# An encoder's SwiGLU by seven products (Strassen): another order of the products, each partial sum copied out

## The chip, the cores and the metric

The kernel runs on one core of a Trainium2 chip. The metric is the device time of one execution in microseconds (us), the median of several runs. TensorE (PE) does matmuls, VectorE (DVE) and ScalarE (ACT) work element by element, GpSimd (POOL) fills buffers, SyncE (SP) issues nearly all loads. Each engine works through its own list of instructions in order and waits for the others by semaphores.

## The reference

Two layers on x of 512 positions by 1024, in float32. Each layer has a mixer (eight retention heads and four differential-attention heads) and a SwiGLU; the change is in the latter.

```python
for l in range(DEPTH):                      # DEPTH = 2
    h = rms_norm(x, attn_norm_g[l])
    proj = h @ w_in[l]                      # 1024 -> 3584
    ...                                     # retention heads, attention heads
    x = x + jnp.concatenate([ret, da], axis=-1) @ w_out[l]

    h = rms_norm(x, ffn_norm_g[l])
    x = x + (jax.nn.silu(h @ w_gate[l]) * (h @ w_up[l])) @ w_down[l]   # 1024 -> 2816 -> 1024
return x
```

## The kernel before, in words

**Two parts for each number.** Matmuls run on float32 rounded to `F32R`. To keep the precision, each operand is split into `hi` (a cast on ACT) and `lo` (the rest, a subtraction on DVE), and a product takes three matmuls: hi by hi, hi by lo, lo by hi. `mm3` (lines 197 to 200) does so for 512 columns. Weights are loaded by SP into one of three `raw` buffers, then split into one of three pairs of buffers with the tags `hi` and `lo` (`NHL = 3`, `parts`, line 171).

**The SwiGLU.** Positions lie along the columns (two halves, H1 and H2, of C = 256 columns each), features along the 128 partitions. The 2816 inner features are 22 units of 128. Groups of units are listed in `FFN` (line 34): after the gate and up products of a group, its part of w_down is applied in a *sweep* over the eight output tiles (`for m in range(KT)`, line 785), and each is added to x (`residual`, line 626). The activations of a group's units are kept till its sweep is done, as pairs in buffers of the tags `h`, `mix` or `rn`.

**Plain units** (the group (0, 4)): `gate_up` computes gate and up with `mm3`. After each, `combine(i)` computes for two of the eight contraction tiles the sums and differences that the seven products need of the normed x, and splits them: b11, b21, b22, t1 to t4. They stay in buffers of `mix`, `qk`, `w` and `dv` to the layer's end.

**Seven-product units** (all others): `seven` treats gate and up of a unit as a 2 by 2 block matrix (gate and up; first and second half of the 1024 contraction rows), times a 2 by 2 block matrix (halves of the contraction; halves of the columns). Seven block products instead of eight are done. The weights come as two loads, `a` (g1 and u2) and `b` (g2 and u1). DVE makes four differences from them: s3 and s1 (in one buffer, s31), s2 and s4 (s24). All are split: s31, then `a`, then g2, then s24. A product is twelve matmuls of 256 columns (`product`, line 736): four contraction tiles by three. The sums run up in three banks of PSUM: `pa` takes g1, s2, s3 and u2 on top of each other, `pb` takes g2, `pc` takes s1 and then s4. What `pa` holds in between is needed too, so ACT and DVE read it (lines 747 to 755) before the next product goes on top. `seven` is a generator; the loop at line 778 interleaves one unit's steps with the next one's by its `yield`s.

**What sets the order.** The kernel is built with `schedule_with_timeline_sim=True`: a planner puts each engine's instructions into an order before the run, by the order of the program, by its own idea of when inputs are ready, and by which buffers are free; it hands the buffers of a tag out. So the order on PE is near to the one written, but products are interleaved. On the chip the order is fixed.

Of the kernel before, what the change touches and what calls it, by code (L numbers as in the profile page):

```python
# [30 lines left out]
FIRST = [("dk", 0), ("dq", 0), ("dk", 1), ("dq", 1)]  # L31
SINGLE = [(n, m) for n in ("dk", "dq") for m in (2, 3)] + [(n, m) for n in ("rk", "rq", "rg") for m in range(4)]

FFN = [(0, 4), (4, 9), (9, 14), (14, 18), (18, FT)]
PLAIN = FFN[0][1]

PAIRS = [0, 0, 1, 0, 1, 2, 0, 1, 2, 3, 1, 2, 3, 2, 3, 3]
# [9 lines left out]
PRM_N = 88  # L47

CST_DIST, CST_DPOS, CST_DNEG, CST_QPOS = 0, 896, 1280, 1664
CST_ID, CST_ONES, CST_BONES, CST_KPOS = 2176, 2304, 2432, 2560  # L50
CST_N = 2564


@with_exitstack
def encoder_kernel(ctx: ExitStack, tc: tile.TileContext, xT, wfirst, wsingle, wvv, wout, wgu, wdn, prm, lam, cst, outT):
# [11 lines left out]
    def nm(s):  # L67
        uid[0] += 1
        return f"{s}{uid[0]}"
# [76 lines left out]
        return sq  # L146

    def round_ones():
        for n, o in (("ones_r", CST_ONES), ("bones_r", CST_BONES)):
            consts[n] = cpool.tile([P, P], F32R, name=n)  # L150
            nc.vector.tensor_copy(consts[n], cst_sb[:, o : o + P])

    eps_sb = cpool.tile([P, 1], F32, name="eps_sb")
    nc.vector.memset(eps_sb, EPS)
# [39 lines left out]
    def chunk(*a, **kw):  # L194
        return split_chunk(*load_chunk(*a, **kw))
# [69 lines left out]
    def prepare_small():  # L265
        lg = cpool.tile([P, 48], F32, name="lg")
        func(lg, prm_sb[:, PRM_DEC : PRM_DEC + 48], AF.Exp)
        nc.vector.tensor_scalar(lg, lg, -1.0, None, op0=ALU.mult)
        lam_sb = big("lam")
        nc.sync.dma_start(lam_sb, lam)  # L270
        lamn = cpool.tile([P, DEPTH], F32, name="lamn")
        for l in range(DEPTH):
            dots = small("dots", 2)
            for i in range(2):
                o = l * 4 * HD + 2 * i * HD
                prod = spool.tile([P, HD], F32, tag="prod", name=nm("prod"), bufs=2)
                nc.vector.tensor_tensor_reduce(prod, lam_sb[:, o : o + HD], lam_sb[:, o + HD : o + 2 * HD], 1.0, 0.0, ALU.mult, ALU.add, dots[:, i : i + 1])
            ex = small("lamex", 2)
            func(ex, dots, AF.Exp)

            nc.vector.tensor_scalar(lamn[:, l : l + 1], ex[:, 1:2], ex[:, 0:1], -LAM_INIT[l], op0=ALU.subtract, op1=ALU.add)
        gq = cpool.tile([P, DEPTH, DH], F32, name="gq")
        gd = cpool.tile([P, DEPTH], F32, name="gd")
        for l in range(DEPTH):
            for h in range(DH):
                nc.vector.tensor_scalar(gq[:, l, h : h + 1], prm_sb[:, PRM_QG + l : PRM_QG + l + 1], -0.5 * HD ** -0.5 / SLOPES[h], None, op0=ALU.mult)
            nc.vector.tensor_scalar(gd[:, l : l + 1], prm_sb[:, PRM_DG + l : PRM_DG + l + 1], 1.0 - LAM_INIT[l], None, op0=ALU.mult)
        wk = cpool.tile([P, DEPTH, 4, RH], F32, name="wk")
# [12 lines left out]

    def layer(l, n1, h, x_src, first_raw):
# [410 lines left out]
        def split_in(raw, hi, lo, n=1024):  # L713
            nc.scalar.copy(hi, raw[:, :n])  # L714
            nc.vector.tensor_tensor(lo, raw[:, :n], f32(hi), op=ALU.subtract)  # L715
            return [(hi[:, i * T : (i + 1) * T], lo[:, i * T : (i + 1) * T]) for i in range(n // T)]
# [4 lines left out]
        def seven(ff, act, tag, bufs):  # L721
            a, b = load_chunk(wgu[l, ff, 0])[0], load_chunk(wgu[l, ff, 1])[0]
            s31, s24 = (tpool.tile([P, 1024], F32, tag="ah", name=nm("s"), bufs=NAH) for _ in range(2))
            u1 = b[:, T:]
            nc.vector.tensor_tensor(s31[:, :T], u1, a[:, :T], op=ALU.subtract)
            nc.vector.tensor_tensor(s31[:, T:], u1, a[:, T:], op=ALU.subtract)  # L726
            nc.vector.tensor_tensor(s24[:, :T], a[:, :T], s31[:, T:], op=ALU.subtract)
            nc.vector.tensor_tensor(s24[:, T:], b[:, :T], s24[:, :T], op=ALU.subtract)
            s3, s1 = split_in(s31, *parts())
            g1, u2 = split_in(a, *parts())  # L730
            (g2,) = split_in(b, big("g2h", F32R), big("g2l", F32R), T)
            s2, s4 = split_in(s24, wide(), wide())

            pa, pb, pc = (bank() for bank in (acc_bank, sc_bank, out_bank))

            def product(ps, w, r, start):
                for k in range(4):
                    L, R = cut(w, slice(None), slice(k * P, (k + 1) * P)), comb[k][r]
                    for i, (x1, x2) in enumerate(((0, 0), (0, 1), (1, 0))):
                        nc.tensor.matmul(ps[:, :C], L[x1], R[x2], start=start and k + i == 0, stop=k == 3 and i == 2, skip_group_check=True)  # L740

            g, u, v = big("g"), big("u"), big("v")
            product(pc, s1, "t1", True)
            yield
            product(pa, g1, "b11", True)
            product(pb, g2, "b21", True)
            nc.scalar.copy(v[:, H1], pb[:, :C])
            nc.vector.tensor_tensor(g[:, H1], pa[:, :C], v[:, H1], op=ALU.add)  # L748
            yield
            product(pa, s2, "t2", False)  # L750
            nc.scalar.copy(v[:, H2], pa[:, :C])  # L751
            yield
            product(pa, s3, "t3", False)
            nc.scalar.copy(u[:, H1], pa[:, :C])
            nc.vector.tensor_tensor(u[:, H2], pc[:, :C], u[:, H1], op=ALU.add)
            yield
            product(pa, u2, "t4", False)
            product(pc, s4, "b22", False)
            nc.vector.tensor_tensor(g[:, H2], pc[:, :C], v[:, H2], op=ALU.add)  # L759
            func(g, g, AF.Silu)  # L760
            nc.vector.tensor_tensor(u[:, H1], pa[:, :C], g[:, H1], op=ALU.mult)  # L761
            nc.vector.tensor_tensor(u[:, H2], u[:, H2], g[:, H2], op=ALU.mult)
            act.append(split(u, tag, bufs))

        for a0, a1 in FFN:
            act, last = [], a1 == FT
            if a1 <= PLAIN:
                for ff in range(a0, a1):
                    act.append(gate_up(ff, *(("mix", NMIX) if ff < 2 else ("rn", 4))))
                    combine(ff)  # L770
            else:
                units = []
                for ff in range(a0, a1):
                    tag = ("h", 8) if not last else ("mix", NMIX) if ff < a0 + 2 else ("rn", 4)
                    units.append(seven(ff, act, *tag))
                next(units[0])
                next(units[0])
                for i, unit in enumerate(units):
                    then = units[i + 1] if i + 1 < len(units) else iter([0, 0])
                    next(unit)  # L780
                    next(then)
                    next(unit)
                    next(then)
                    next(unit, None)
            for m in range(KT):
                w = chunk(wdn[l, m][:, a0 * P : a1 * P], (a1 - a0) * P)
                if last and l + 1 == DEPTH and m == KT - 1:

                    for t, queue in ((H1, nc.sync), (H2, nc.scalar)):
# [9 lines left out]
                if last and l + 1 < DEPTH:  # L799
                    residual(m, x[m], ps, n3, h3, PRM_AG + 8 * (l + 1))  # L800
                    nc.sync.dma_start(xscr[m], x[m])
                else:
                    residual(m, x[m], ps, None, None, None)
                    if last:
                        nc.sync.dma_start(outT[m], x[m])
        return n3, h3
# [15 lines left out]
def _constants():  # L822
    import numpy as np

    p = np.arange(P, dtype=np.float32)[:, None]
    ndist = -np.abs(p + 384 - np.arange(896, dtype=np.float32)[None])
    d = np.arange(384, dtype=np.float32)[None] - P - p
    j = np.arange(C, dtype=np.float32)
    qpos = np.tile(np.concatenate([C - j, j + 1])[None], (P, 1))
    blk = (np.arange(P) // HD)[:, None] == (np.arange(P) // HD)[None]  # L830
    kpos = np.concatenate([C - 1 - p, C - 1 - P - p, p, P + p], 1)
    return np.concatenate(
        [ndist, np.maximum(d, 0), np.maximum(-d, 0), qpos, np.eye(P), np.ones((P, P)), blk, kpos], 1
    ).astype(np.float32)


# [74 lines left out]
```

## Time and profile before

| | |
|---|---|
| median of 3 runs | 1313.53 us (1311.27 to 1313.73) |
| the profiled execution: its time, its span | 1314.86 us, 1313.1 us |
| PE, DVE, ACT, POOL busy, share of the span | 96%, 74%, 52%, 1% |
| granted TensorE clock, mean | 0.996 |
| DMA moved, mean rate | 120.30 MB, 92 GB/s |
| layer 0: plain units and start of their sweep | 294.5 to 347.3 us |
| layer 0: groups of seven-product units with their sweeps | 347.3 to 637.7 us |
| layer 1: the same two | 944.0 to 998.2 us, 998.2 to 1290.6 us |

A row of the timeline reads: start, duration, engine, line of the kernel, operation, what is written <- what is read, shapes, count, and in brackets how long the engine had been idle before and who ended it. The records of matmuls overlap: one starts while the one before is drained, so the distance between two starts says what a matmul costs. A row of the waits view reads: who waited, for whom, total us, times, longest. In windows: busy us of each engine, its instructions, granted clock, share of DMA, GB/s.

### The profile page before, as it was taken

To read this page: it belongs to the slowest core of one execution; us is meant where nothing else is said; L and a number is where in the kernel's file an instruction comes from. 1 tells how busy PE (TensorE), PEld (TensorE's weight loads), DVE (VectorE), ACT (ScalarE), POOL (GpSimd) and SP (SyncE) were. 2 spreads that over 40 slices of the span, in tenths; PEclk is the share of its full clock that TensorE was granted. 3 is DMA by queue.
4 is the path that set the end of the run, shared out by engine and by line. 5 is a ranking of instruction groups with operands and counts; after the bars stand their busy time and mean duration, and the time that the engine had idled before them with its cause. 6 is when DMAs were issued, how large, how long until landed. Compare 5 with 4: busy or idle time off the path is not lost.

```text
span 1313.1 us, 19158 instructions
## 1 busy us (share of the span) xinstructions
PE 1263.8 (96%) x7516; PEld 1100.5 (84%) x7516; DVE 972.4 (74%) x1634; ACT 683.4 (52%) x1138; POOL 17.3 (1%) x38
## 2 busy tenths in 40 slices
PE   9999999999899999998999999999999999999998
PEld 8888998778797888988888888977878889888787
DVE  6899769779874766767659988686897757566664
ACT  6878656455343443434548875654653434334342
POOL 1000000000000000000000000000000000000000
PEclk9999999999999999999999999999999999999999
DMA  7212224122323324232443122230314233232323
GB/s 269 86 49 81 65 67 126 49 68 74 116 85 92 97 73 121 73 105 80 144 130 92 37 85 76 88 106 32 105 40 133 79 95 113 61 116 66 113 74 103
DMA packets 41562, 120.30 MB, mean 92 GB/s; under 512 B 4736, under 2 KB 4992, under 8 KB 41344
## 3 DMA queue, kind: packets, MB, share of 16 engines
q1 hardware_dynamic: 41040, 118.64, 29.1%
q8 instruction: 59, 0.97, 0.3%
q10 hardware_dynamic: 432, 0.44, 0.1%
q14 instruction: 31, 0.25, 0.1%
HBM read 114.87 MB, written 4.19 MB: 91 GB/s over the span
## 4 chain that ended last, share of the span: by engine, by line
PE 38%; DVE 6%; DMA 3%; ACT 2%; issue 2%; DVEq 0%; ACTq 0%; SPq 0%
PE acc L740 6%; PE acc L198 5%; PE acc L199 5%; PE acc L200 5%; DMA raw<-in_wgu 3%; PE o L740 3%; PE o L198 2%; PE o L199 2%; PE o L200 2%; PE sc L198 2%; PE sc L199 1%; PE sc L200 1%; PE sc L392 1%; PE sc L740 1%; DVE lo L715 1%
## 5 line engine op out<-in xcount | busy, mean ns | idle before, releaser
L187 ACT CAST hi<-raw 128x1024 fp32r<-128x1024 f32 (+2 forms) x171 | 143.4, 850 | 185.0 <-PE acc L199 53.4
L191 DVE TENSOR_TENSOR lo<-raw,hi 128x1024 fp32r<-128x1024 f32 (+2 forms) x172 | 166.2, 972 | 69.9 <-ACT hi L187 69.2
L198 PE MATMUL acc<-h,hi 128*128 128x512 f32 x411 | 161.8, 395 | 0.7 <-DVE u L761 0.4
L199 PE MATMUL acc<-h,hi 128*128 128x512 f32 x411 | 161.0, 392 | 0.0
L200 PE MATMUL acc<-h,lo 128*128 128x512 f32 x411 | 160.7, 392 | 0.0
L198 PEld LDWEIGHTS acc<-h,hi 128*128 128x128 f32 x411 | 77.1, 188 | 19.8 <-ACT hi L187 2.4
L200 PEld LDWEIGHTS acc<-h,lo 128*128 128x128 f32 x411 | 77.2, 188 | 16.0
L199 PEld LDWEIGHTS acc<-h,hi 128*128 128x128 f32 x411 | 77.2, 188 | 15.5 <-DVE h L216 0.4
L740 PE MATMUL acc<-hi,hi 128*128 128x256 f32 x288 | 83.3, 289 | 2.1 <-ACT v L751 2.0
L740 PE MATMUL acc<-lo,hi 128*128 128x256 f32 x288 | 81.3, 282 | 0.0
L740 PE MATMUL acc<-hi,lo 128*128 128x256 f32 x288 | 81.2, 282 | 0.0
L106 ACT ACTIVATE g<-g 128x512 f32<-128x512 f32 x44 | 27.8, 632 | 83.6 <-DVE g L759 81.8
L740 PE MATMUL acc<-hi,s 128*128 128x256 f32 x288 | 61.2, 295 | 7.4 <-DVE g L748 7.4
L714 ACT CAST hi<-s 128x1024 fp32r<-128x1024 f32 x36 | 37.8, 1051 | 55.3 <-DVE s L726 34.2
L715 DVE TENSOR_TENSOR lo<-raw,hi 128x1024 fp32r<-128x1024 f32 x36 | 43.9, 1220 | 27.8 <-ACT hi L714 27.8
L714 ACT CAST hi<-raw 128x1024 fp32r<-128x1024 f32 x36 | 37.7, 1048 | 51.5 <-issue 29.5
L740 PE MATMUL acc<-bh,hi 128*128 128x256 f32 x144 | 43.6, 303 | 17.0 <-ACT hi L714 17.0
L740 PEld LDWEIGHTS acc<-hi,hi 128*128 128x128 f32 x288 | 54.6, 190 | 5.1 <-ACT v L751 4.6
L198 PE MATMUL sc<-h,hi 128*128 128x512 f32 x147 | 57.7, 396 | 0.6 <-ACT h L215 0.6
L740 PE MATMUL o<-b,s 128*128 128x256 f32 x432 | 57.6, 283 | 0.0
L199 PE MATMUL sc<-h,hi 128*128 128x512 f32 x147 | 57.4, 391 | 0.0
L200 PE MATMUL sc<-h,lo 128*128 128x512 f32 x147 | 57.1, 390 | 0.0
(234 smaller groups left out, 3694.2 us busy)
## 6 DMA issues: line engine op xcount, KB each, us to landing
raw<-in_wgu SPq DMA_DIRECT2D x88, 512.0 KB, 3.6
raw<-in_wsingle SPq DMA_DIRECT2D x32, 512.0 KB, 3.6
raw<-in_wdn SPq DMA_DIRECT2D x48, 256.0 KB, 2.7
raw<-in_wdn SPq DMA_DIRECT2D x32, 320.0 KB, 2.9
raw<-in_wvv SPq DMA_DIRECT2D x16, 512.0 KB, 3.7
raw<-in_wout SPq DMA_DIRECT2D x16, 512.0 KB, 3.6
x<-in_xT SPq DMA_DIRECT2D x15, 256.0 KB, 4.3
raw<-in_wfirst SPq DMA_DIRECT2D x8, 256.0 KB, 5.1
```

The source lines that it names most:

```text
L106: i = nc.scalar.activation(out, src, f, **kw).ins
L187: c = nc.scalar.copy(hi[:, s], raw[:, s])
L191: nc.vector.tensor_tensor(lo[:, s], raw[:, s], f32(hi[:, s]), op=ALU.subtract)
L198: nc.tensor.matmul(out, L[0], R[0], start=start, stop=False)
L199: nc.tensor.matmul(out, L[0], R[1], start=False, stop=False)
L200: nc.tensor.matmul(out, L[1], R[0], start=False, stop=stop)
L392: nc.tensor.matmul(ps, q[m][:, t], k[m][part], start=part == 0, stop=part == 1)
L714: nc.scalar.copy(hi, raw[:, :n])
L715: nc.vector.tensor_tensor(lo, raw[:, :n], f32(hi), op=ALU.subtract)
L740: nc.tensor.matmul(ps[:, :C], L[x1], R[x2], start=start and k + i == 0, stop=k == 3 and i == 2, skip_group_check=True)
```

## The change

- The groups are (0, 4), (4, 12), (12, 18), (18, 22) instead of (0, 4), (4, 9), (9, 14), (14, 18), (18, 22): four sweeps a layer instead of five.
- Order of the splits in `seven`: `a`, then s2 and s4, then s31, then g2. In all but the last group s2 and s4 are split one by one into `mix` buffers and g2 goes to `rn`; in the last group s24 goes to `h` and g2 to `w`, as before.
- Order of the products of a unit: g1, s2, s1, s3, g2, u2, s4 (before: s1, g1, g2, s2, s3, u2, s4), with the next unit's g1 between u2 and s4.
- After g1, after s2 and after s3, ACT copies what `pa` holds straight into the result's buffer (g or u); DVE adds `pb` or `pc` to it there. Before, the result of g2 was copied, and DVE added `pa` and the copy, ahead of s2.
- `combine(i)` is issued one unit later, the last one behind the second tile of the first sweep.
- Where a group has four units, two tiles of w_down weights share one raw buffer: two loads, one cast, one subtraction.
- The matrices of ones come from memsets on POOL instead of the loaded constants (2308 of 2564 constant columns are still loaded); `prod` takes a `w` buffer.

```diff
-FFN = [(0, 4), (4, 9), (9, 14), (14, 18), (18, FT)]
+FFN = [(0, 4), (4, 12), (12, 18), (18, FT)]
 ...
     def round_ones():
-        for n, o in (("ones_r", CST_ONES), ("bones_r", CST_BONES)):
+        o = big("ones")
+        nc.gpsimd.memset(o[:, :P], 1.0)
+        nc.gpsimd.memset(o[:, P : 2 * P], 0.0)
+        for b in (slice(0, HD), slice(HD, P)):
+            nc.gpsimd.memset(o[b, P + b.start : P + b.stop], 1.0)
+        for i, n in enumerate(("ones_r", "bones_r")):
             consts[n] = cpool.tile([P, P], F32R, name=n)
-            nc.vector.tensor_copy(consts[n], cst_sb[:, o : o + P])
+            nc.vector.tensor_copy(consts[n], o[:, i * P : (i + 1) * P])
 ...
+            late = ff >= FFN[-1][0]
+            g1, u2 = split_in(a, *parts())
+            tag2 = ("w", NW) if late else ("rn", 4)
+            if late:
+                s2, s4 = split_in(s24, wide(), wide())
+            else:
+                s2, s4 = (split(s24[:, i * T : (i + 1) * T], "mix", NMIX) for i in range(2))
             s3, s1 = split_in(s31, *parts())
-            g1, u2 = split_in(a, *parts())
-            (g2,) = split_in(b, big("g2h", F32R), big("g2l", F32R), T)
-            s2, s4 = split_in(s24, wide(), wide())
+            (g2,) = split_in(b, big("g2h", F32R, *tag2), big("g2l", F32R, *tag2), T)
 ...
-            g, u, v = big("g"), big("u"), big("v")
+            g, u = big("g"), big("u")
+            product(pa, g1, "b11", True)
+            nc.scalar.copy(g[:, H1], pa[:, :C])
+            yield
+            product(pa, s2, "t2", False)
+            nc.scalar.copy(g[:, H2], pa[:, :C])
             product(pc, s1, "t1", True)
-            yield
-            product(pa, g1, "b11", True)
+            product(pa, s3, "t3", False)
+            nc.scalar.copy(u[:, H2], pa[:, :C])
+            nc.vector.tensor_tensor(u[:, H2], pc[:, :C], u[:, H2], op=ALU.add)
             product(pb, g2, "b21", True)
-            nc.scalar.copy(v[:, H1], pb[:, :C])
-            nc.vector.tensor_tensor(g[:, H1], pa[:, :C], v[:, H1], op=ALU.add)
-            yield
-            product(pa, s2, "t2", False)
-            nc.scalar.copy(v[:, H2], pa[:, :C])
-            yield
-            product(pa, s3, "t3", False)
-            nc.scalar.copy(u[:, H1], pa[:, :C])
-            nc.vector.tensor_tensor(u[:, H2], pc[:, :C], u[:, H1], op=ALU.add)
-            yield
+            nc.vector.tensor_tensor(g[:, H1], pb[:, :C], g[:, H1], op=ALU.add)
             product(pa, u2, "t4", False)
+            yield
             product(pc, s4, "b22", False)
-            nc.vector.tensor_tensor(g[:, H2], pc[:, :C], v[:, H2], op=ALU.add)
+            nc.vector.tensor_tensor(g[:, H2], pc[:, :C], g[:, H2], op=ALU.add)
 ...
                     act.append(gate_up(ff, *(("mix", NMIX) if ff < 2 else ("rn", 4))))
-                    combine(ff)
+                    if ff:
+                        combine(ff - 1)
 ...
                 next(units[0])
-                next(units[0])
                 for i, unit in enumerate(units):
-                    then = units[i + 1] if i + 1 < len(units) else iter([0, 0])
                     next(unit)
-                    next(then)
-                    next(unit)
-                    next(then)
+                    if i + 1 < len(units):
+                        next(units[i + 1])
                     next(unit, None)
+            n = (a1 - a0) * P
             for m in range(KT):
-                w = chunk(wdn[l, m][:, a0 * P : a1 * P], (a1 - a0) * P)
+                both = 2 * n <= 1024
+                if not both or m % 2 == 0:
+                    new = new_chunk(n * (1 + both), 1)
+                    for i in range(1 + both):
+                        nc.sync.dma_start(new[0][:, i * n : (i + 1) * n], wdn[l, m + i][:, a0 * P : a1 * P])
+                    ww = split_chunk(*new)
+                w = cut(ww, slice(None), slice(m % 2 * n, (m % 2 + 1) * n)) if both else ww
 ...
                     residual(m, x[m], ps, None, None, None)
+                    if a1 <= PLAIN and m == 1:
+                        combine(PLAIN - 1)
```

More of the change, by code (lines that the diff above doesn't have):

```diff
@@ L49 @@
 CST_DIST, CST_DPOS, CST_DNEG, CST_QPOS = 0, 896, 1280, 1664
-CST_ID, CST_ONES, CST_BONES, CST_KPOS = 2176, 2304, 2432, 2560
-CST_N = 2564
+CST_ID, CST_KPOS = 2176, 2304
+CST_N = 2308
 @with_exitstack
@@ L275, in prepare_small @@
                 o = l * 4 * HD + 2 * i * HD
-                prod = spool.tile([P, HD], F32, tag="prod", name=nm("prod"), bufs=2)
+                prod = big("prod")[:, :HD]
                 nc.vector.tensor_tensor_reduce(prod, lam_sb[:, o : o + HD], lam_sb[:, o + HD : o + 2 * HD], 1.0, 0.0, ALU.mult, ALU.add, dots[:, i : i + 1])
@@ L740, in product @@
                         nc.tensor.matmul(ps[:, :C], L[x1], R[x2], start=start and k + i == 0, stop=k == 3 and i == 2, skip_group_check=True)
-            g, u, v = big("g"), big("u"), big("v")
-            product(pc, s1, "t1", True)
-            yield
+            g, u = big("g"), big("u")
             product(pa, g1, "b11", True)
-            product(pb, g2, "b21", True)
-            nc.scalar.copy(v[:, H1], pb[:, :C])
-            nc.vector.tensor_tensor(g[:, H1], pa[:, :C], v[:, H1], op=ALU.add)
+            nc.scalar.copy(g[:, H1], pa[:, :C])
             yield
             product(pa, s2, "t2", False)
-            nc.scalar.copy(v[:, H2], pa[:, :C])
-            yield
-            product(pa, s3, "t3", False)
-            nc.scalar.copy(u[:, H1], pa[:, :C])
-            nc.vector.tensor_tensor(u[:, H2], pc[:, :C], u[:, H1], op=ALU.add)
-            yield
-            product(pa, u2, "t4", False)
+            nc.scalar.copy(g[:, H2], pa[:, :C])
+            product(pc, s1, "t1", True)
+            product(pa, s3, "t3", False)
+            nc.scalar.copy(u[:, H2], pa[:, :C])
+            nc.vector.tensor_tensor(u[:, H2], pc[:, :C], u[:, H2], op=ALU.add)
+            product(pb, g2, "b21", True)
+            nc.vector.tensor_tensor(g[:, H1], pb[:, :C], g[:, H1], op=ALU.add)
+            product(pa, u2, "t4", False)
+            yield
             product(pc, s4, "b22", False)
-            nc.vector.tensor_tensor(g[:, H2], pc[:, :C], v[:, H2], op=ALU.add)
+            nc.vector.tensor_tensor(g[:, H2], pc[:, :C], g[:, H2], op=ALU.add)
             func(g, g, AF.Silu)
@@ L829, in _constants @@
     qpos = np.tile(np.concatenate([C - j, j + 1])[None], (P, 1))
-    blk = (np.arange(P) // HD)[:, None] == (np.arange(P) // HD)[None]
     kpos = np.concatenate([C - 1 - p, C - 1 - P - p, p, P + p], 1)
     return np.concatenate(
-        [ndist, np.maximum(d, 0), np.maximum(-d, 0), qpos, np.eye(P), np.ones((P, P)), blk, kpos], 1
+        [ndist, np.maximum(d, 0), np.maximum(-d, 0), qpos, np.eye(P), kpos], 1
     ).astype(np.float32)
```

## The prediction, made before the changed kernel was run

> **What bounds the kernel now.** I read the page first: TensorE (PE) is busy nearly throughout.
>
> ```profile
> span 1313.1 us, 19158 instructions
> PE 1263.8 (96%) x7516; PEld 1100.5 (84%) x7516; DVE 972.4 (74%) x1634; ACT 683.4 (52%) x1138; POOL 17.3 (1%) x38
> ```
>
> The change leaves the number of matmuls alone, so I can gain only where PE waits. To find where, I cut the span by stage (windows, all engines): the four plain units with the first w_down sweep's start, then the seven-product units with their sweeps, per layer. Under them the same two long windows, matmuls of line 740 alone.
>
> ```profile
> core 0: us, PE busy (x) PEld busy (x) DVE busy (x) ACT busy (x) POOL busy (x), PEclk, DMA share, GB/s
> 294.50:347.30 52.80, 50.43 (x218) 39.99 (x217) 46.89 (x86) 26.63 (x46) 0.00 (x0) 1.00 0.30 90
> 347.30:637.70 290.40, 273.18 (x1867) 250.10 (x1866) 194.23 (x297) 118.83 (x184) 1.51 (x3) 0.99 0.30 91
> 944.00:998.20 54.20, 51.60 (x219) 41.57 (x217) 47.58 (x87) 27.39 (x46) 0.00 (x0) 0.97 0.29 88
> 998.20:1290.60 292.40, 274.34 (x1867) 250.30 (x1866) 193.81 (x296) 118.52 (x184) 0.00 (x0) 0.99 0.30 90
> ```
> ```profile
> 347.30:637.70 290.40, 192.20 (x1512) 186.84 (x1511) 0.99 0.30 91
> 998.20:1290.60 292.40, 192.97 (x1512) 187.04 (x1511) 0.99 0.30 90
> ```
>
> A busy sum hides part of a stall, as a matmul's record overlaps the next. Better is the step from start to start when PE waits for nothing. PE's timeline gives it twice, and the two kinds of stall beside it: first the plain unit's end, then a group's start, then the inner of a group.
>
> ```profile
> 327.72 0.39 PE L199 MATMUL sc<-lo,hi 128*128 128x512 f32 x1
> 327.95 0.40 PE L200 MATMUL sc<-hi,lo 128*128 128x512 f32 x1
> 328.99 0.50 PE L198 MATMUL o<-hi,hi 128*128 128x512 f32 x1 [0.64 <-ACT hi L215]
> 329.56 0.40 PE L198 MATMUL sc<-hi,hi 128*128 128x512 f32 x1
> 331.56 0.50 PE L199 MATMUL o<-lo,hi 128*128 128x512 f32 x1 [1.60 <-DVE lo L216]
> ...
> 351.35 0.28 PE L740 MATMUL acc<-bl,hi 128*128 128x256 f32 x1
> 351.47 0.28 PE L740 MATMUL acc<-bh,lo 128*128 128x256 f32 x1
> 354.03 0.58 PE L740 MATMUL acc<-hi,s 128*128 128x256 f32 x1 [2.28 <-DVE g L748]
> ...
> 382.91 0.28 PE L740 MATMUL acc<-hi,lo 128*128 128x256 f32 x1
> 384.25 0.39 PE L740 MATMUL acc<-bh,hi 128*128 128x256 f32 x1 [1.06 <-ACT hi L714]
> ```
>
> Steps: 0.23 us at 512 columns (0.227 on average), 0.12 at 256. A window of seven-product units needs 1512 x 0.12 + 355 x 0.227 = 262.0 us; it takes 290.4 and 292.4, so 28.4 and 30.4 are lost. The plain windows need 218 and 219 x 0.227 = 49.5 and 49.7 and lose 3.3 and 4.5. In all 66.6 us; no change here can return more. The waits view says to whom:
>
> ```profile
> PE acc L740 <- ACT hi L714: 17.0, 16, 1.1
> PE acc L740 <- DVE g L748: 7.4, 4, 2.3
> PEld acc L740 <- DVE lo L715: 4.9, 8, 1.3
> PEld acc L740 <- ACT v L751: 4.6, 11, 0.5
> ```
>
> **The change, part by part.**
>
> *1. Order of products and splits.* ScalarE's (ACT) timeline shows the cause of the 16 waits:
>
> ```profile
> 383.15 1.04 ACT L714 CAST hi<-raw 128x1024 fp32r<-128x1024 f32 x1 [1.81 <-issue]
> 384.10 0.37 ACT L754 COPY u<-acc 128x256 f32<-128x256 f32 x1
> ```
>
> The cast of the next unit's `a` (g1, u2) begins at 383.15, 0.24 after the last matmul of s3 has started at 382.91: it takes a `hi` buffer which that product held. There are three pairs (NHL = 3) and a unit fills two, s31 first; a unit's `a` thus waits for the s31 parts of the unit before, and g1 is wanted at once. Each costs 1.34 - 0.12 = 1.22 us, 16 of them 19.5. After the change `a` is split first, s31 follows. s31's last reader, s3, is the third product in sequence, and behind it come g2, u2, the next g1, s4 and s2 before another s1 needs the pair: five products x 12 x 0.12 = 7.2 us, against a cast of 1.05 and a subtraction of 1.22. Price 0, cover 7.2; without cover the old 1.22 comes back (rival 2). I book -19.5.
>
> *2. Copies in place of the add.* Before, s2 waits until g2's result is copied and added (line 748). After, every partial sum in `pa` is copied out (g1, s2, s3), and the next product into that bank waits for one copy. The nearest row is a copy that PE waited for:
>
> ```profile
> 442.31 0.28 PE L740 MATMUL acc<-hi,s 128*128 128x256 f32 x1
> ...
> 442.55 0.28 PE L740 MATMUL sc<-bl,g2h 128*128 128x256 f32 x1
> 443.05 0.38 PE L740 MATMUL acc<-hi,hi 128*128 128x256 f32 x1 [0.23 <-ACT v L751]
> ```
>
> From the last matmul into the bank to the next one into it: 0.74 us. In each of the three places another product lies between (s4, s1, g2), 1.44 + 0.12 = 1.56 us, so a copy may come 0.82 late for nothing. One 1024-wide cast ahead of it in ACT's queue takes 0.95 (383.15 to 384.10 above): 0.13 of stall. Bounds: 0 with ACT free, 0.13 with a cast ahead; I take the middle, 0.06, for 108 copies (3 x 18 units x 2 layers) = 6.5. The eleven old waits on line 751 go, of 443.05 - 442.55 - 0.12 = 0.38 each, 4.0: +2.5 (between -4 and +10). The u add (line 755's role) is in the way of s4 alone, four products later; g's adds and the silu are in no product's way until the bank's next turn.
>
> *3. Group starts.* There the add cost 2.44 (354.03 - 351.47 - 0.12) in the longest of four, 8 in all (7.4 of PE idle and four hidden 0.16). After, a first g1 has no s4 behind it: up to 0.74 of copy, six starts x 0.7 = 4. Net -4. The clock adds to it: each of three long stalls is followed by a slow stretch.
>
> ```profile
> 353.90:357.30 3.40, 3.27 (x15) 3.27 (x16) 3.01 (x5) 1.18 (x3) 0.00 (x0) 0.50 0.19 31
> 982.00:985.40 3.40, 3.40 (x10) 2.62 (x9) 3.37 (x6) 2.14 (x4) 0.00 (x0) 0.51 0.00 0
> 1244.80:1248.20 3.40, 3.40 (x18) 3.40 (x18) 2.62 (x4) 1.36 (x3) 0.00 (x0) 0.50 0.22 48
> ```
>
> The granted clock is 0.50 for 3.4 us; 15 and 18 narrow matmuls run there instead of 28, 10 wide ones instead of 15: 1.6, 1.2 and 1.1 us lost. With the stalls gone, -3.9. The Trainium skill, "TensorE: Matmul & The Clock Gate", Part 1, has the gate close after an idle window of about 3.4 us; here PE had been idle 2.28 us. By the page's window these stalls would not have closed it, there would be nothing to return, and the sum would be 3.9 higher; the measured rows decide.
>
> The other start waits, for subtractions on VectorE (DVE; line 715, 11 places, 7.3 us from start to start), are of a first unit whose parts come late. With s2 and s4 in `mix` and g2 in `rn`, the first unit's parts of group (4, 12) must now wait for the plain group's last sweep step, whose activations hold these buffers: one cast of 0.62, one subtraction of 0.69, with g1 (1.44) and, if it is taken ahead, s1 as cover. Between all returned and none, I take half: -3.5.
>
> *4. combine moved.* At 328 to 331.6 PE waits for both parts of the fourth plain unit, because DVE works through combine(3) first (the subtraction `lo<-u` starts at 330.81):
>
> ```profile
> 330.48 0.42 DVE L697 TENSOR_TENSOR ta<-b,ta 128x256 f32<-128x256 f32 x1
> 330.81 0.69 DVE L216 TENSOR_TENSOR lo<-u,hi 128x512 fp32r<-128x512 f32 x1
> ```
>
> Stalls 0.81 + 1.77 a layer, 5.2. After, combine(3) stands behind the second w_down tile, with six more 12-matmul tiles (2.7 us each) as cover for its 4 us or so of DVE work; without cover g1 of the first unit would wait for it. About 0.6 a layer stays: -4.
>
> *5. Groups 4-8-6-4.* One sweep less a layer: eight residual adds, eight loads and casts fewer, which are hidden now, and one start and one tail less. A tail shows 0.2 to 0.9 us stalls behind lines 187 and 215; I take 1.5 for each group: -3. In a group of eight PE spends 24 x 0.227 = 5.4 us a tile on a 512 KB load of 3.6 us (below), so loads stay hidden.
>
> *6. Paired w_down weights, constants from memsets, `prod`.* A pair is two 256 KB loads of 2.7 us each, on the same SP queue, into one 1024-wide buffer for 5.4 us of PE; the raw buffers hold twice as many tiles ahead. First tiles wait for both: under the last unit's products. The memsets (POOL, idle) and copies stand where the first 28 us of matmuls cover them. 0, within 1 us either way.
>
> ```profile
> raw<-in_wgu SPq DMA_DIRECT2D x88, 512.0 KB, 3.6
> raw<-in_wdn SPq DMA_DIRECT2D x48, 256.0 KB, 2.7
> ```
>
> Sum: -19.5 + 2.5 - 4 - 3.9 - 3.5 - 4 - 3 = -35.4. The profiled execution took 1314.86 us; that gives 1279.5, and as the median of the runs shown (1313.53) is 1.3 lower, 1278. The best end by the bounds: copies -4 instead of +2.5, all 7.3 and all 5.2 of parts 3 and 4 returned, 1267; the range goes 9 lower, for start and tail waits that the listed ones do not name (66.6 is what there is in all).
>
> **The rivals.**
>
> *1. DVE becomes the bound.* In one steady unit it is nearly as full as PE:
>
> ```profile
> 371.50:382.95 11.45, 10.39 (x86) 10.19 (x85) 8.96 (x15) 5.73 (x9) 0.00 (x0) 1.00 0.28 93
> ```
> ```profile
> L715 DVE TENSOR_TENSOR lo<-s,hi 128x1024 fp32r<-128x1024 f32 x1 | 1.2, 1224 | 0.5 <-ACT hi L714 0.5
> L216 DVE TENSOR_TENSOR h<-u,h 128x512 fp32r<-128x512 f32 x1 | 0.7, 693 | 0.7 <-ACT h L215 0.7
> L725 DVE TENSOR_TENSOR s<-raw,raw 128x512 f32<-128x512 f32 x1 | 0.7, 693 | 0.6 <-DMA raw<-in_wgu 0.6
> L761 DVE TENSOR_TENSOR u<-acc,g 128x256 f32<-128x256 f32 x1 | 0.4, 426 | 0.7 <-ACT g L106 0.7
> ```
>
> 8.96 busy, +0.16 for s2 and s4 as two subtractions (2 x 0.69 for 1.22), against 84 x 0.12 = 10.08 of PE. The idle 0.5 + 0.7 + 0.7 is there because nothing else can run; if it stays, a unit takes 11.0 and the 30 units that are not a group's first lose 0.9 each: 1305. With half of it filled a unit takes 10.1, and nothing is lost; in between, 1292. For it: the narrow margin. Against: `a` is now released early, so the next raw weights are there to fill these holes.
>
> *2. The pairs stay short:* the planner, which orders each engine's work and gives out buffers, hands s31's old pair to the next `a` and s31 waits for u2. Then 19.5 comes back: 1297. Against it: even then u2 ends three products (4.3 us) before s1.
>
> *3. Nothing moves:* rivals 1 and 2 in part and the copies at 0.2 each eat the gain: 1311 to 1316.
>
> *4. Slower: the copies wait in ACT's order.* 108 copies stand on PE's path; if casts that themselves wait are put ahead of them, each stalls. It decides from (35.4 + 6.5) / 108 = 0.39 us a copy, that is a copy 1.21 late; at 0.45 the time is 1320. Against: ACT is busy 5.73 of 11.45 above. The Trainium skill, "Perfetto Trace Analysis", Optimizing Tensor Performance, wants independent matmul groups in different banks, so that emptying one overlaps the next; three dependent products in one bank are the opposite, and only the product put between obeys it.
>
> **How the numbers follow.** Forecast 0.62 (1278; its own range 1262 to 1290), rival 1 0.14, rival 2 0.10, rival 3 0.05, rival 4 0.09. A measurement of this kernel can tell about 0.2%, 2.6 us. Faster 0.62 + 0.14 + 0.10 = 0.86, same 0.05, slower 0.09. The range 1258 to 1302 leaves out rivals 3 and 4, the far end of rival 1 and a little below: 0.19.
>
> **What would show it.** Right: the 16 waits on `hi` L714 gone, inner units of about 10.2 to 10.4 us, copies (lines 751 and 754 in their new places) at most 0.2 of PE idle each, no 0.50 clock after a group start, and the plain window near 50 us. Wrong: DVE busy over 9.8 of a unit (rival 1), PE waiting for s31's parts (2), or for copies by more than 0.39 (4). The forecast fails most easily by the planner's order, which no row of before shows.

## The result, and the profile after

The changed kernel takes 1271.4 us (median of four, 1270.15 to 1271.85) against 1313.63 of the kernel before (1311.27 to 1313.84): ratio 0.968 [0.966, 0.970], 42 us less. The forecast was 1278, so the whole came out 7 us better. Its parts did not come out as booked: one fell short by some 13 us and others brought more, so that the sum came so near is in part luck.

The page of the kernel after:

```profile
span 1268.9 us, 19110 instructions
PE 1246.7 (98%) x7516; PEld 1097.9 (87%) x7516; DVE 959.7 (76%) x1614; ACT 680.2 (54%) x1134; POOL 17.9 (1%) x42
```

PE has the same 7516 matmuls; the time came out of the gaps between them. The windows of the same stages (the mixer of layer 0; plain units; seven-product units; what lies between the layers; the same two of layer 1; the end):

```profile
0.00:299.20 299.20, 294.25 (x1601) 247.73 (x1602) 236.37 (x435) 192.73 (x340) 9.63 (x26) 0.99 0.28 93
299.20:349.40 50.20, 49.72 (x219) 40.72 (x218) 47.44 (x83) 27.24 (x44) 0.00 (x0) 1.00 0.30 98
349.40:621.00 271.60, 266.01 (x1868) 248.56 (x1868) 188.55 (x293) 118.49 (x188) 1.56 (x3) 1.00 0.31 101
621.00:926.20 305.20, 303.50 (x1663) 256.76 (x1662) 242.44 (x418) 193.81 (x329) 6.72 (x14) 1.00 0.26 85
926.20:976.40 50.20, 49.73 (x219) 40.72 (x218) 47.43 (x83) 27.23 (x44) 0.00 (x0) 1.00 0.30 98
976.40:1247.70 271.30, 265.59 (x1867) 248.45 (x1866) 188.33 (x293) 118.41 (x188) 0.00 (x0) 1.00 0.30 99
1247.70:1268.90 21.20, 17.89 (x90) 14.94 (x88) 9.11 (x15) 2.31 (x3) 0.00 (x0) 1.00 0.27 100
```

Set beside the windows of before, the span's 44.2 us are: 18.8 and 21.1 from the seven-product windows (290.4 to 271.6, 292.4 to 271.3), 2.6 and 4.0 from the plain ones, 1.1 from between the layers, 1.3 from the end, and 4.7 *lost* in the mixer of layer 0 (294.5 to 299.2), where the change was meant to cost nothing. A seven-product window needs 262.0 us, so 9.6 and 9.3 are still lost there, of 28.4 and 30.4.

What is left, by the waits view of the kernel after:

```profile
PE o L751 <- ACT hi L719: 12.0, 14, 1.1
PE o L203 <- DVE sq L513: 2.2, 1, 2.2
PE sc L397 <- DVE mx L401: 1.5, 4, 0.5
```

The first row is the surprise: the wait for a cast into a `hi` buffer, which the new order was to end, is still there 14 times (before: 16, 17.0 us). It stands at s1 (bank `o`) instead of at g1 (bank `acc`). Twelve of the 14 are in the groups (12, 18) and (18, 22) of both layers; the other two, of 0.43 us each, belong to the first s1 of the group of eight, which PE takes ahead among the plain units' sweep (at 344.2 and 971.2). Inside the window of the group of eight there is none. That window, and one unit of the last group:

```profile
349.40:426.40 77.00, 76.99 (x636) 76.40 (x636) 66.42 (x109) 41.64 (x72) 0.00 (x0) 1.00 0.33 110
...
592.10:603.54 11.44, 10.37 (x86) 10.16 (x84) 8.27 (x13) 5.67 (x9) 0.00 (x0) 1.00 0.31 93
```

In the group of eight PE is busy 76.99 of 77.00. In the last group a unit takes 11.44 us, as long as the unit of 11.45 shown of before. PE's timeline gives the reason. First the group of eight, where s3 of a unit ends at 367.17 and s1 of the next starts at 369.45; then the last group, where the same two stand next to each other:

```profile
367.17 0.28 PE L751 MATMUL acc<-hi,lo 128*128 128x256 f32 x1
...
368.01 0.28 PE L751 MATMUL acc<-bh,hi 128*128 128x256 f32 x1
...
369.33 0.28 PE L751 MATMUL acc<-bh,lo 128*128 128x256 f32 x1
369.45 0.28 PE L751 MATMUL o<-hi,hi 128*128 128x256 f32 x1
...
592.00 0.28 PE L751 MATMUL acc<-hi,lo 128*128 128x256 f32 x1
593.35 0.39 PE L751 MATMUL o<-hi,hi 128*128 128x256 f32 x1 [1.07 <-ACT hi L719]
```

And ACT in the two places:

```profile
367.43 1.05 ACT L719 CAST hi<-s 128x1024 fp32r<-128x1024 f32 x1 [1.17 <-PE acc L751]
368.38 0.37 ACT L762 COPY u<-acc 128x256 f32<-128x256 f32 x1
...
592.25 1.04 ACT L719 CAST hi<-s 128x1024 fp32r<-128x1024 f32 x1 [2.92 <-PE acc L751]
593.21 0.37 ACT L762 COPY u<-acc 128x256 f32<-128x256 f32 x1
```

In both, the cast of the next unit's s31 waits for the end of s3, 0.25 or 0.26 us after the start of its last matmul: two of the three pairs hold the `a` of this unit and of the next, and the third is the one that s3 has just read. So `a` before s31 does not free a pair earlier; it only decides which product has to wait. In the group of eight the planner put part of g2 and the next unit's g1 (1.44 us) between s3 and s1, 2.28 us in all, and the cast is hidden. In the last group it had placed g1 ahead of s3, nothing is between, and s1 waits 593.35 - 592.00 - 0.12 = 1.23 us.

The mixer's loss is one wait and a slow stretch behind it (timeline, then window, of the kernel after):

```profile
265.87 0.40 PE L140 MATMUL aux<-lo,bones_r 128*128 128x512 f32 x1
268.49 0.67 PE L203 MATMUL o<-hi,hi 128*128 128x512 f32 x1 [2.22 <-DVE sq L513]
```
```profile
268.60:272.10 3.50, 3.50 (x9) 2.73 (x10) 1.25 (x2) 0.62 (x1) 0.00 (x0) 0.51 0.02 5
```

From start to start 2.62 - 0.23 = 2.39 us are lost, and then 9 wide matmuls run in 3.5 us where 15 would: some 1.5 more. That is 3.9 of the 4.7.

### The profile page after: what moved, and what is told of

The parts are those of the page before. It is cut to its first block, busy times and chain, and to the rows that moved or that the text cites. A ratio compares the mean times of both kernels' runs of the same rounds, so it can differ in the third digit from the quotient of the medians.

```text
span 1268.9 us, 19110 instructions
## 1 busy us (share of the span) xinstructions
PE 1246.7 (98%) x7516; PEld 1097.9 (87%) x7516; DVE 959.7 (76%) x1614; ACT 680.2 (54%) x1134; POOL 17.9 (1%) x42
## 4 chain that ended last, share of the span: by engine, by line
PE 92%; DVE 4%; ACT 2%; issue 1%; DMA 1%; ACTq 0%; SPq 0%
PE acc L751 16%; PE acc L203 11%; PE acc L205 11%; PE acc L204 11%; PE o L751 8%; PE o L205 4%; PE o L203 4%; PE o L204 4%; PE sc L751 4%; PE sc L203 4%; PE sc L205 4%; PE sc L204 4%; PE sc L397 2%; PE o L498 1%; PE sc L482 1%; ACT hi L719 1%
## 5 line engine op out<-in xcount | busy, mean ns | idle before, releaser
L751 PE MATMUL acc<-hi,hi 128*128 128x256 f32 x400 | 113.7, 284 | 0.0
L751 PE MATMUL acc<-lo,hi 128*128 128x256 f32 x400 | 113.1, 283 | 0.0
L751 PE MATMUL acc<-hi,lo 128*128 128x256 f32 x400 | 113.0, 283 | 0.0
L751 PEld LDWEIGHTS acc<-hi,hi 128*128 128x128 f32 x400 | 76.5, 191 | 0.7 <-ACT u L762 0.2
L751 PEld LDWEIGHTS acc<-lo,hi 128*128 128x128 f32 x400 | 76.6, 191 | 0.3
L751 PEld LDWEIGHTS acc<-hi,lo 128*128 128x128 f32 x400 | 76.6, 191 | 0.0
L220 ACT CAST hi<-s 128x512 fp32r<-128x512 f32 x56 | 34.8, 621 | 62.6 <-PE o L751 32.9
L720 DVE TENSOR_TENSOR lo<-s,hi 128x1024 fp32r<-128x1024 f32 x36 | 43.9, 1220 | 27.5 <-ACT hi L719 27.5
L204 PE MATMUL sc<-h,hi 128*128 128x512 f32 x164 | 63.6, 390 | 0.0
L203 PE MATMUL sc<-h,hi 128*128 128x512 f32 x164 | 63.1, 392 | 0.3 <-ACT hi L192 0.3
L106 ACT ACTIVATE sc<-sc,mx 128x512 f32<-128x512 f32 x64 | 46.0, 719 | 18.3 <-DVE mx L401 17.9
```

Of the source, the lines that this page charges most:

```text
L106: i = nc.scalar.activation(out, src, f, **kw).ins
L203: nc.tensor.matmul(out, L[0], R[0], start=start, stop=False)
L204: nc.tensor.matmul(out, L[0], R[1], start=False, stop=False)
L220: nc.scalar.copy(hi, src)
```

## The experiments

Every kernel is compared with the kernel before, run beside it on the same chip; the changed kernel stands at 0.968 on this scale.

**The order of the products alone undone.** Products, copies and `yield`s of before, with the new splits, buffers, groups and the rest:

```diff
+            product(pc, s1, "t1", True)
+            yield
             product(pa, g1, "b11", True)
-            nc.scalar.copy(g[:, H1], pa[:, :C])
+            product(pb, g2, "b21", True)
+            nc.scalar.copy(v[:, H1], pb[:, :C])
+            nc.vector.tensor_tensor(g[:, H1], pa[:, :C], v[:, H1], op=ALU.add)
             yield
             product(pa, s2, "t2", False)
...
```

> The changed kernel with the products, copies and yields of before (s1, g1, g2, s2, s3, u2, s4; g2's result copied and added ahead of s2); splits, buffers, groups, combine and pairs stay changed. Theory A (the order of the products, in which only a copy stands between two products of one bank, carries most of the gain): about 1297 to 1305, with the waits for line 748's add back at group starts. Theory B (the order of the splits carries it, by freeing the pairs): at most 1280. Theory C (groups, combine and pairing carry it): 1272 to 1278.

Measured: 1287.72 us, ratio 0.980 [0.977, 0.982]. The value lies between what theories A and B gave, and above C, so none was right in size: the order of products is worth 16 us by the medians. The waits view says where:

```profile
PE acc L751 <- DVE u L772: 5.2, 20, 0.3
PE o L751 <- ACT hi L719: 9.4, 10, 1.1
PE acc L751 <- ACT v L762: 2.5, 3, 0.9
```

The hi waits are fewer than in the changed kernel, but waits for results in the banks come in: line 772 reads the last sum in `pa`, line 762 is the copy of s2's sum. The wait for the add, which theory A expected at group starts, is not in the list.

**The order of the splits alone undone.**

```diff
-            g1, u2 = split_in(a, *parts())
+            s3, s1 = split_in(s31, *parts())
+            g1, u2 = split_in(a, *parts())
+            (g2,) = split_in(b, big("g2h", F32R, *tag2), big("g2l", F32R, *tag2), T)
             ...                     # s2 and s4 as after
-            s3, s1 = split_in(s31, *parts())
-            (g2,) = split_in(b, big("g2h", F32R, *tag2), big("g2l", F32R, *tag2), T)
```

> The changed kernel with the splits in the order of before (s31, a, g2, s2 and s4); all else stays changed. Theory A: within 6 us of 1271, as the planner follows readiness more than the written order of splits. Theory B: 1290 or more, with 1.2 us waits for hi in each inner unit of the group of eight, which now has none.

Measured: 1296.24, 0.986 [0.984, 0.988]: the split order is worth 25 us, the size that theory B gave. Its waits:

```profile
PE acc L751 <- ACT hi L719: 9.4, 10, 1.1
PE acc L751 <- ACT g L759: 4.5, 12, 0.8
PE sc L751 <- ACT g2h L719: 3.5, 5, 0.9
PE o L751 <- DVE g L769: 2.6, 5, 0.6
```

The hi wait is back in front of bank `acc` (g1), but theory B's sign is not there: it expected 1.2 us in each inner unit of the group of eight, and the waits for hi are 9.4 us in all, less than the 12.0 of the changed kernel. What the 25 us go to are other things that come late: the copies (line 759 is the copy of s2's sum), g2's cast, the add of s4's sum (line 769), and smaller ones. So the new order of splits does not gain by fewer waits for a pair. Each half of the change needs the other: with the old splits the copies cost what rival 4 feared, in small (4.5 us); with the new ones they cost nothing.

**The kernel before with the new products and one split moved.** To see whether these two edits are the whole:

```diff
-            s3, s1 = split_in(s31, *parts())
             g1, u2 = split_in(a, *parts())
+            s3, s1 = split_in(s31, *parts())
             (g2,) = split_in(b, big("g2h", F32R), big("g2l", F32R), T)
             s2, s4 = split_in(s24, wide(), wide())
             ...                     # and the products, copies and yields of after
```

> The kernel before with two things of the change alone: the new order of products with its copies, and a split ahead of s31 (s31 then g2, s2 and s4 behind). Buffers, groups, combine, single w_down tiles and loaded ones are those of before. Theory (order of products and of splits are the change; each undone cost 16 and 25 us): 1274 to 1282. Rival (s2 and s4 in mix and g2 in rn, ahead of s31, are what the order of splits needs): 1290 or more, with waits for hi or for s2's parts in inner units.

Measured: 1289.24, 0.980 [0.978, 0.981]; the expectation was missed and its rival nearly hit. 26 of the 42 us come, and these are its longest waits:

```profile
PE o L740 <- ACT hi L714: 8.6, 8, 1.1
PE acc L740 <- ACT g L748: 5.2, 10, 0.7
PE acc L740 <- DVE u L760: 5.0, 4, 1.8
```

The plain units' waits of before are there as well. The other 16 us need what this kernel lacks: s2, s4 split ahead of s31 and g2 in `mix`, `rn` buffers, the groups, the pairs. Which of these carries how much was tried for the groups and the pairs alone (next, and below).

**The groups of before.** `FFN = [(0, 4), (4, 9), (9, 14), (14, 18), (18, FT)]`.

> The changed kernel with the groups of before, (4, 9), (9, 14), (14, 18), (18, 22). Theory A: 1273 to 1278: one more start and tail a layer, some 1.5 us each, and a few waits more or less. Theory C: 1285 or more. If the group of eight is free of waits because it is long, the groups of five show 1.2 us waits in their inner units; if it is free because it is the first after the plain units, the group (4, 9) is free of them too and (9, 14) is not.

Measured: 1273.88, 0.969 [0.967, 0.971]: 2.5 us by the medians, within what two such comparisons can tell. Within the group (4, 9) there is no hi wait in layer 0 and one of 0.45 us in layer 1; (9, 14) has one of 0.80 us in each layer. So a group need not be of eight to be almost free of them. That being the first after the plain units is what frees a group fits this, but rests on these few waits.

**combine at its old place.**

```diff
-                    if ff:
-                        combine(ff - 1)
+                    combine(ff)
...
-                    if a1 <= PLAIN and m == 1:
-                        combine(PLAIN - 1)
```

> The changed kernel with combine(i) behind unit i at once, as before. Theory: the stalls of 0.8 and 1.8 us at the end of the plain units come back in each layer, with a stretch of half clock in some: 1276 to 1279. Rival (paired weights cover the plain units' tail by themselves): within 1.5 us of 1271.

Measured: 1270.53, 0.967 [0.965, 0.969]. With the pairs in place, moving `combine` gave nothing.

**No pairs of w_down weights.** `both = False`.

> The changed kernel with one w_down tile for each raw buffer in the groups of four as well. With combine in its old place the stalls at the end of the plain units did not come back, so something else removed them. Theory (pairs: a raw buffer and a hi/lo pair that hold two tiles give PE twice as many matmuls that do not need the last unit): the plain windows show stalls of 1 to 3 us each again, 1274 to 1278. Rival (it was the buffers or the order elsewhere): within 1.5 us of 1271.

Measured: 1273.85, 0.968 [0.967, 0.970]. That is 2.5 more by the medians, a little below the range expected. The ratios alone don't separate it from the changed kernel; the trace does. The plain units' end has two stalls again, with `combine` moved:

```profile
332.93 0.39 PE L203 MATMUL sc<-hi,hi 128*128 128x512 f32 x1
333.77 0.50 PE L204 MATMUL o<-lo,hi 128*128 128x512 f32 x1 [0.45 <-DVE lo L221]
```
```profile
PE o L205 <- DVE lo L196: 2.7, 2, 1.4
```

They are not quite those of before, which both waited for the activations. Here the first does (line 221), and the second waits for the split of the fourth w_down tile (line 196). The timeline shows three tiles begun and left for the last unit's activations, as in the kernel before: there are three hi/lo pairs, one tile in each. With two tiles in a pair, six are at hand, and PE works on them while DVE gets to the rest.

**The ones from loaded constants again** (to find the mixer's wait):

```diff
-        o = big("ones")
-        nc.gpsimd.memset(o[:, :P], 1.0)
         ...
+            nc.vector.tensor_copy(consts[n], cst_sb[:, o : o + P])
```

> The changed kernel with the matrices of ones cut from the loaded constants again, without the four memsets and the buffer they take; prod stays in a w buffer. The changed kernel waits 2.4 us at 266 us for line 513 (the last retention pair's norm), which the kernel before did not. Theory: memsets and buffer shift the planner's order in the mixer, so the wait and the half clock behind it go: 1267 to 1268.5. Rival (the wait comes from another part of the change, such as prod in a w buffer): within 1 us of 1271, the wait still there.

Measured: 1270.36, 0.966 [0.964, 0.967], and the wait is still there. So the ones are not its cause. But it is not followed by a slow stretch here, though PE and ACT do their instructions in exactly the order of the changed kernel. Timeline and window:

```profile
265.92 0.40 PE L140 MATMUL aux<-lo,bones_r 128*128 128x512 f32 x1
268.54 0.50 PE L198 MATMUL o<-hi,hi 128*128 128x512 f32 x1 [2.23 <-DVE sq L508]
```
```profile
268.60:272.10 3.50, 3.50 (x16) 2.89 (x17) 1.30 (x2) 0.62 (x1) 0.00 (x0) 1.00 0.02 5
```

**`prod` in a buffer of its own**, the other edit that touches the mixer:

```diff
-                prod = big("prod")[:, :HD]
+                prod = spool.tile([P, HD], F32, tag="prod", name=nm("prod"), bufs=2)
```

> The changed kernel with prod in two small buffers of its own again instead of a w buffer. Up to the FFN of the first layer its instructions then stand in the order of before. Theory (prod in a w buffer shifts the planner's order in the mixer, and so the 2.4 us wait for line 513 at 266 us and, in some executions, 1.6 us of half clock behind it arise): the wait goes, the first plain unit starts 3 to 5 us earlier, 1267 to 1269. Rival (the order is the same, but the wait comes back from late data): 1271.

Measured: 1277.13, 0.971 [0.969, 0.973]: 6 us worse, where 2 to 4 better was expected. The profiled execution had a granted clock of 0.655, so where the time goes is read from a later kernel with the same edit; of this trace only the order of the instructions is used.

**s31 in `h` buffers in the last group**, so that its cast need not wait for s3 there:

```diff
-            s3, s1 = split_in(s31, *parts())
+            s3, s1 = split_in(s31, *((wide(), wide()) if late else parts()))
```

> The changed kernel with the parts of s31 in two buffers of the tag h in the last group, which has them to spare; elsewhere the three hi/lo pairs as they are. In the last group s1 waits 1.23 us for the cast into hi, three times a layer. Theory (pairs short: the next a holds the third pair, so s31's cast waits for s3 to end): these six waits go, 1263 to 1265. Rival (ACT's order: the cast and the copy of s3 stand one behind the other and nothing else is left for PE, whatever the buffers): within 2 us of 1271.

Measured: 1273.35, 0.968 [0.966, 0.969]. In the last group the three waits for the cast go, 3.7 us a layer from start to start, but three shorter ones come (for s31's subtraction and a copy, 1.4 us), so that some 2.3 are gained there, less than expected. And the gain was lost elsewhere (waits view):

```profile
PE sc L751 <- ACT g2h L719: 2.3, 1, 2.3
```

In layer 1's group of eight, which had no such wait, one new wait for g2's cast came with a slow stretch behind it, some 6 us in all. The edit is not in that group; the planner's order there changed all the same.

**s31 in `h` for every other unit of (12, 18) and for the last group, layer 1 alone:** the condition becomes `l and (late or ff >= 12 and ff % 2)`.

> The changed kernel with s31's parts in buffers of the tag h in the last group and in every other unit of the group (12, 18), in the second layer alone, so that the order of all that comes before is unchanged. Theory (three hi/lo pairs are one too few): the waits for line 719's cast go in these two groups of the second layer, about 3.4 + 3.7 us, 1264 to 1266, and the first layer keeps its own. Rival (ACT's order): 1270 or more.

Measured: 1265.97, 0.963 [0.962, 0.965], in the theory's range. Of the eight waits left, seven lie in layer 0 and one in front of layer 1's group of eight, which the edit does not touch; the windows show the last group of layer 0 as after and the same group of layer 1 free:

```profile
PE o L751 <- ACT hi L719: 6.2, 8, 1.1
```
```profile
570.60:612.00 41.40, 38.18 (x313) 37.57 (x312) 28.04 (x42) 19.39 (x31) 0.53 (x1) 1.00 0.28 90
1195.30:1240.00 44.70, 43.99 (x339) 42.38 (x338) 29.36 (x45) 19.24 (x31) 0.00 (x0) 1.00 0.26 83
```

PE idles for 3.2 us in the first window and for 0.7 in the second (which is cut 3.3 us wider). That shows that a free pair for s31 is what these units lack. In size the theory was lucky: from start to start the two groups and the sweep behind them give 3.7 us, not 7, and some 1.6 of the rest is the mixer's slow stretch, which is not in this trace (the wait of 2.22 us is, and the clock behind it is 1.00).

**Both together:** `prod` of its own, and `h` as in the kernel just shown.

> Both: prod in buffers of its own, and s31's parts in h buffers in the second layer. Theory: the gains are at different places and add, 1260 to 1263. Rival (the planner's order moves elsewhere): over 1265.

Measured: 1271.67, 0.967 [0.965, 0.969]; 1260 to 1263 was missed. The mixer's wait is gone (the plain units start at 294.6 instead of 299.2), so `prod` was its cause: in a `w` buffer it moves the planner's order in the mixer. The order shows it directly: up to 302 us, in the plain units, ACT and PE do the same instructions in the same order here, in the kernel with `prod` alone and in the kernel before, while in the changed kernel and the one with loaded ones another order stands from 33 us (ACT) and 40 us (PE) on. But the groups of eight lost 5.2 us in layer 0 and 6.8 in layer 1. ACT's and PE's timeline in layer 0, and the slow stretch behind:

```profile
355.85 0.62 ACT L719 CAST g2h<-raw 128x512 fp32r<-128x512 f32 x1 [3.55 <-DMA raw<-in_wgu]
356.38 1.04 ACT L719 CAST hi<-s 128x1024 fp32r<-128x1024 f32 x1
357.32 0.36 ACT L762 COPY u<-acc 128x256 f32<-128x256 f32 x1
...
356.52 0.39 PE L751 MATMUL sc<-bh,g2h 128*128 128x256 f32 x1 [1.40 <-ACT g2h L719]
...
357.73 0.40 PE L751 MATMUL sc<-bh,g2l 128*128 128x256 f32 x1 [0.70 <-DVE g2l L720]
```
```profile
357.90:361.30 3.40, 3.40 (x17) 3.40 (x18) 2.86 (x5) 0.06 (x1) 0.00 (x0) 0.51 0.00 0
```

The cast of the third unit's g2 waits 3.55 us for its load, and because ACT works in order, the cast of s31 and the copy of s3 behind it wait as well, though they could have run (s3's last matmul started at 353.64). This is the mechanism of rival 4. The kernel with `prod` alone has the same order on ACT and PE through both groups of eight, with this cast of g2 in the same place:

```profile
489.10 0.62 ACT L719 CAST g2h<-raw 128x512 fp32r<-128x512 f32 x1 [1.19 <-DMA raw<-in_wgu]
492.38 1.05 ACT L719 CAST hi<-s 128x1024 fp32r<-128x1024 f32 x1 [2.66 <-PE acc L751]
```

So the order that costs here stood there too; how much of its 6 us it cost, its trace at 0.655 of the clock cannot tell.

**The same, with one rule of order for the planner:** g2's cast of a unit must stand behind the copy of s3 of the unit two before, and `h` for s31 in both layers.

```diff
+            s3, s1 = split_in(s31, *((wide(), wide()) if (late or ff >= 12 and ff % 2) else parts()))
...
+            c = nc.scalar.copy(g2[0], b[:, :T])
+            if ff - 2 in copied:
+                tc.add_manual_dep(c.ins, copied[ff - 2], order, reason="copies ahead of casts")
...
-            nc.scalar.copy(u[:, H2], pa[:, :C])
+            copied[ff] = nc.scalar.copy(u[:, H2], pa[:, :C]).ins.name
```

> The changed kernel with prod in its own buffers, s31's parts in h buffers in the last group and every other unit of (12, 18) in both layers, and one rule for the planner: g2's cast of a unit stands behind the copy of s3 two units before in ScalarE's order. In e13_all (own prod) and in the second layer of e7_late_h PE waited 2.4 to 3.4 us near the start of the group of eight for g2's cast, which stood ahead of that copy in ScalarE's queue and waited for its weights to land. Theory (that order is the fault, not prod or the h buffers): the waits and the half clock behind them do not come, and the gains add: 3.3 us in the mixer, 5.4 in each layer, 1257 to 1260. Rival (with more buffers free the planner finds other bad orders, or the weights are late anyway): 1266 or more.

Measured: 1258.89, 0.957 [0.955, 0.959], as expected: 57 us below the kernel before beside it, and 12 (medians) to 15 (ratios) below the changed one. ACT's timeline in the same place, and the longest row of its waits on PE:

```profile
355.94 1.05 ACT L719 CAST hi<-s 128x1024 fp32r<-128x1024 f32 x1 [1.55 <-PE acc L757]
356.89 0.36 ACT L768 COPY u<-acc 128x256 f32<-128x256 f32 x1
357.54 0.62 ACT L746 CAST g2h<-raw 128x512 fp32r<-128x512 f32 x1
```
```profile
PE sc L397 <- DVE mx L401: 1.9, 5, 0.5
```

The cast of g2 now comes last of the three. The longest wait left in the seven-product units is one of 0.6 us. Two things differ from the kernel with both edits, the rule and the `h` buffers in layer 0. In the two profiled executions, from start to start, the groups of eight, where no `h` buffer was added, give 5.1 and 7.4 us; the later groups of layer 0 with their sweep give 3.8; and the mixer takes 1.9 back.

## Why the prediction was right, and which of its terms were not

The sign and the size hold, but not for the reason that carried most of the sum. Of the prediction's own signs, DVE's load, the copies, the clock behind group starts and the plain windows came as said; the 16 waits did not go, inner units of the last group stayed at 11.44, and PE waits for s31's parts, which was rival 2's sign. The parts compare as follows.

*1. Order of splits (booked -19.5): the mis-sized term.* 16 weight loads of PE still wait for a cast of line 719; from start to start they cost 14.6 us in all, 13.5 of it in the seven-product windows, so that some 5 to 6 us came back at the place named. The step that failed is "five products x 12 x 0.12 = 7.2 us" of cover. It took the pair that s3 frees to be wanted only by the next s1, five products later in the program's order. But that pair is wanted at once by the *cast* of s31, and the planner had drawn the next g1 ahead of s3, so that s1 came next: cover 0. (s3 is the fourth product of a unit, not the third; the count of five is right.) Rival 2 had the mechanism, that s31 waits for a pair; its "against" (4.3 us of products between) was wrong for the same reason, and only its buffer was another: s3's and not u2's. Even so the split order is worth 25 us when it alone is undone, and not by waits for a pair, of which the old order has fewer: without it copies, g2's cast and an add come late. That the old order of splits would cost this way is not in the prediction.

*2. Copies (booked +2.5): better than booked, near the low end of -4.* The waits view of after has no row of PE for the copies, and PE's weight loads have one of 0.2 us. The eleven old waits (4.0) went. The Trainium skill, "Perfetto Trace Analysis", Optimizing Tensor Performance, wants independent groups in different banks; what the trace adds is that three dependent products in one bank cost nothing as long as one product of another bank stands between them.

*3. Group starts and half clock (-4, -3.9, -3.5): more than booked.* No half clock follows a group's start or the plain units' end any more, the 2.28 us add is gone, and no wait for a subtraction of the seven-product splits (line 720 now) is in the list of either PE view. I had kept 4 us for copies at the starts and half of the 7.3 of line 715; neither appears.

*4. combine moved (-4): the right size for the wrong cause.* The plain windows gave 6.6 in both layers together, 1.1 of it the half clock at 982 us that part 3 had booked. But with `combine` at its old place the time is the same, and without the pairs two stalls, of 0.61 and 1.54 us from start to start, are there in each layer. So the pairs, booked at 0 in part 6, are enough by themselves. I had read "late behind combine(3)" out of DVE's order and left out of the count that PE had only three w_down tiles at hand, all begun, while it waited.

*5. One group less (-3):* 2.5 by the medians when undone, though the ratios alone would allow none.

*6. `prod`, booked at 0 within 1 us:* wrong. It costs 4.7 in the mixer, and its removal alone made the whole 6 us slower, with an order on ACT that cost 5.2 and 6.8 us in the groups of eight of the kernel with both edits. A buffer's tag is an input of the planner, and the order of things far away hangs on it.

*Sum.* In the seven-product windows 30.3 was booked (19.5 - 2.5 + 4 + 2.8 + 3.5 + 3; 1.1 of the 3.9 for the half clock belongs to a plain window) and 39.9 came: about 13 less from part 1, and some 23 more from the others. Of these 23, copies and group starts make some 14 (6.4 for the copies, 4 for the adds, 3.8 for line 715); the rest lies in short waits in tails and in matmuls that run a little late behind each stall, which the list did not name. The plain windows gave 1.5 more than the 5.1 booked, the mixer took 4.7, the rest gave 2.4. Two errors of opposite sign thus nearly cancelled.

*The rivals.* DVE (rival 1) did not bind: busy 66.42 of 77.00 in the group of eight, with PE at 76.99; the idle time that had been there because nothing could run was filled. Rival 4 did not decide the changed kernel, but came up as soon as other edits moved ACT's order, for 5 to 7 us a group of eight.

## What to carry to other kernels

When a change is to end a wait for a buffer, follow the buffer, not the operand: write down who reads it last, who is written into it next, and what the engine has to do between these two in the order it really has (the timeline, not the program). Where a planner makes the order, a small edit in one place can cost or save several us in another; compare all stages after each, and where one order is needed, say so to the planner. An engine that works in order should not have an instruction that waits for a load ahead of copies that empty PSUM.

## What the runs showed of the hardware

The half clock followed idle stretches of some 1.6 to 2.3 us, and not always. After 2.22 us of idle in the mixer (one execution) PE ran at a granted clock of 0.51 for about 3.4 us; in the kernel with the loaded ones the same idle of 2.23 us, in the same place and with the same order of instructions on PE and ACT, was followed by 1.00. In the kernel with both edits 1.40 and 0.70 us of idle, with two matmuls between, were followed by 0.51 for 3.4 us. In the kernel before, six stalls had 1.56 to 2.28 us of idle; the half clock came behind three of them (2.28, 1.60 and 1.84, those that the prediction shows) and not behind the other three (1.60 at 331.6, 1.56 at 593.1, 1.70 at 1004.4), so 1.60 stands on both sides. The Trainium skill, "TensorE: Matmul & The Clock Gate", Part 1, has an idle window of about 3.4 us close the gate; here less was enough. Why the same idle is followed by a slow stretch in one execution and not in another, these runs don't settle.
